# The last stage of a hybrid decoder step: tokens on partitions in five tiles, with the gate's weights as the moving operand

## The chip, the cores and the metric

One NeuronCore of a Trainium2 chip runs the whole program. The time is device microseconds (us) of one launch. Three runs of the kernel before took 2060.99, 2060.96 and 2056.74 us, with a median of 2060.96 us. A fourth, profiled run took 2059.39 us; the first to the last instruction in its trace span 2057.6 us.

The engines are named as in the profile: PE multiplies matrices (PEld is its weight load), DVE works on vectors, ACT applies functions and copies, POOL here issues gathers and some transfers, and SP issues most transfers. Each engine takes its instructions in program order, so an instruction that waits also holds whatever is queued behind it on that engine.

## What is computed

The layer runs on T = 544 tokens (512 of a prompt and 32 of decoding samples) of width 1024, all in 32-bit floats. Cut to the parts that matter here, the reference is:

```
x = x + merged @ w_out                                  # two token mixers, merged
x = x + peer_ffn(rmsnorm(x, g_ffn), ...)                # experts, 16384 of one neuron each
ple_gate = sigmoid(rmsnorm(x, g_ple) @ w_ple_gate)      # 1024 x 1024
x = x + (p @ w_ple) * ple_gate                          # p has 256 columns
y = rmsnorm(x, g_final)
```

The last three lines are the last stage, the one that the change rewrites. A matrix product of two 32-bit operands is made as three faster products: each operand is split into a rounded high part and the rest (`split`, L121: a copy by ACT to the high part, a subtraction by DVE for the low one), and high times high, low times high and high times low are added up.

## The kernel before, in words

The mixers take the first 650 us of the trace. After them, one scheduled block (line 835) holds everything else. Its program order on each engine is not the order of the source: a scheduler in the compiler's front end reorders the block's instructions by simulated times, so a change anywhere in the block can move instructions elsewhere in it.

The block has four parts. **Queries**: x1, the sum of the input and the mixers' output, lies in SBUF with channels on partitions (`x1[128, 8, 544]`). It is stored to a DRAM buffer `x1s` (L870, five transfers from POOL), normed into `hf`, split, and multiplied with 16 chunks of the query weights (L916). Of the last 128 prompt tokens and the 32 samples a token-major copy is made for the experts that are gathered (`token_rows`, L902 and L905: PE transposes of `hf`, which ACT copies into `htok` and `hsam`). Each query chunk is scored against 128 keys (`psc`, L937), and DVE picks the top 16 of each row (`top16`, from L892 on). **Gates** turn these into a dense matrix of expert weights for the first 384 tokens. **Products**: 128 blocks of experts, counted by j, each with an up product (`ublock`, L966 to L969), an activation times a gate (`act*gg`, L1180), a split into `wgh` and `wgl`, and 18 matmuls of 512 columns into three accumulators `pacc` (L1194). **Gathered experts**: for the other 160 tokens, POOL gathers rows of single experts (L1108) and DVE adds them up (`accg`, L1126), in between the products.

The last stage before, L1219 to L1313, works with channels on partitions, on two halves of 272 tokens each. x1 is loaded back (L1222, tied to the load of block 118). The first three token tiles of the experts' sum are copied out of PSUM, turned by 24 PE transposes (L1249) and added to x1 by DVE (L1251). `p @ w_ple` is 96 matmuls of 272 columns (L1265). For each half a norm is made over partitions (`rms_rstd`, L92: squares by ACT, sums by DVE, matmuls with ones and a broadcast), the normed half is split into `fh` and `fl`, and the gate is 192 matmuls of 272 columns (L1303) with the weights as the stationary operand. A chunk of weights `wpg` serves one half, so the eight chunks are loaded and split twice (16 calls of `wload`). After each chunk come the sigmoid, the product with `pw` and the sum; after each half, the last norm and four output transfers (L1313).

## Time and profile before

| | before |
|---|---|
| median of three runs | 2060.96 us |
| profiled run | 2059.39 us |
| span of its trace | 2057.6 us |
| PE busy | 1976.0 us, 96% |
| DVE busy | 1706.7 us, 83% |
| ACT busy | 1028.8 us, 50% |
| POOL busy | 513.9 us, 25% |
| from the last matmul of the experts (1957.2) to the end | 100.4 us |

All times in the trace count from the start of the span. PEclk is the clock granted to PE as a share of full speed: 1.00 is the upper of its two levels (2.4 GHz), 0.50 the lower (1.2 GHz), and numbers in between are mixes over the stretch. Where matmuls follow each other, the price of one is the distance from start to start, not its own duration, since they overlap.

### The profile page before, as it was taken

How to read it: one execution, taken by the hardware profiler on the slowest of the kernel's cores; microseconds unless marked ns; L12 is line 12 of the kernel's file. 1: busy time of each engine (PE TensorE's matmuls, PEld its weight loads, DVE VectorE, ACT ScalarE, POOL GpSimd, SP SyncE). 2: the span in 40 equal slices, each digit the busy share in tenths (PEclk: the TensorE clock that was granted, in tenths of full speed). 3: DMA queues.
4: the chain of work that ended last, by engine and by line, in shares of the span. 5: the costliest groups of instructions: out<-in, count | busy, mean ns of one | idle time of the engine just before them, and what ended most of it. 6: DMA issues, size and time to landing. Idle time of an engine off the chain costs nothing.

```text
span 2057.6 us, 34634 instructions
## 1 busy us (share of the span) xinstructions
PE 1976.0 (96%) x12292; PEld 1833.5 (89%) x12292; DVE 1706.7 (83%) x4582; ACT 1028.8 (50%) x1717; POOL 513.9 (25%) x503
## 2 busy tenths in 40 slices
PE   6899999999998999999999799999999999999986
PEld 6898988988998999999999688888888888888886
DVE  7687988886566799999999888888888888887877
ACT  5657577663534446766666333333333333343374
POOL 0001010000000001213332455543433334543500
PEclk9999999999999999999999899999999999999998
DMA  4334443445755238999999899999999998999843
GB/s 161 113 103 137 149 153 125 166 147 176 264 191 190 79 94 202 255 265 351 388 369 325 309 351 353 334 356 344 345 339 349 346 331 328 342 337 328 296 135 105
DMA packets 188364, 516.10 MB, mean 251 GB/s; under 512 B 18464, under 2 KB 71712, under 8 KB 188064
## 3 DMA queue, kind: packets, MB, share of 16 engines
q1 hardware_dynamic: 131952, 311.11, 43.5%
q0 software_dynamic: 56240, 202.80, 28.9%
q8 instruction: 96, 1.57, 0.3%
q14 instruction: 76, 0.62, 0.1%
HBM read 453.64 MB, written 60.20 MB: 250 GB/s over the span
## 4 chain that ended last, share of the span: by engine, by line
PE 86%; DVE 5%; DMA 4%; ACT 3%; issue 3%; POOL 0%; SPq 0%; DVEq 0%; ACTq 0%; POOLq 0%
PE pacc L1194 26%; PE pj L165 15%; PE pu L967 8%; PE pu L966 8%; PE pu L969 8%; PE pj L916 5%; PE pg L1083 3%; PE pj L1303 2%; DMA lraw<-in_eu 1%; PE pma L348 1%; PE pmb L553 1%; PE pmb L544 1%; ACT whi L122 1%; PE psc L937 1%; DMA usp<-lraw 1%
## 5 line engine op out<-in xcount | busy, mean ns | idle before, releaser
L966 PE MATMUL pu<-hh,whi 128*128 128x384 f32 x1024 | 346.0, 338 | 2.6 <-ACT act L977 2.6
L967 PE MATMUL pu<-hl,whi 128*128 128x384 f32 x1024 | 346.3, 338 | 0.0
L1108 POOL DMA_INDIRECT rows<-in_ev,idxs x160 | 218.0, 1362 | 267.8 <-DVE accg L1126 228.3
L123 DVE TENSOR_TENSOR wlo<-wraw,whi 128x1024 fp32r<-128x1024 f32 x172 | 210.0, 1222 | 74.6 <-ACT whi L122 65.7
L1108 POOL DMA_INDIRECT rows<-in_eur,idxs x160 | 202.1, 1263 | 248.1 <-DVE jk L1116 213.7
L122 ACT ACTIVATE whi<-wraw 128x1024 fp32r<-128x1024 f32 x172 | 181.7, 1057 | 164.2 <-PE pj L165 84.9
L1126 DVE SCALAR_TENSOR_TENSOR accg<-rows,wts,accg 128x1024 f32<-128x1024 f32 x158 | 202.5, 1281 | 21.1 <-DMA rows<-in_ev,idxs 20.9
L1194 PE MATMUL pacc<-whi,wgl 128*128 128x512 f32 x768 | 197.5, 392 | 6.1 <-DVE wgl L123 6.1
L969 PE MATMUL pu<-hh,wlo 128*128 128x384 f32 x1024 | 202.0, 336 | 0.0
L1194 PE MATMUL pacc<-whi,wgh 128*128 128x512 f32 x768 | 198.2, 394 | 2.5 <-ACT wgh L122 2.5
L966 PEld LDWEIGHTS pu<-hh,whi 128*128 128x128 f32 x1024 | 192.5, 188 | 5.8 <-ACT act L977 3.2
L1194 PE MATMUL pacc<-wlo,wgh 128*128 128x512 f32 x768 | 195.9, 390 | 0.0
L967 PEld LDWEIGHTS pu<-hl,whi 128*128 128x128 f32 x1024 | 192.7, 188 | 2.6
L122 ACT ACTIVATE whi<-vraw 128x1024 fp32r<-128x1024 f32 x128 | 134.8, 1054 | 113.9 <-PE pacc L1194 86.4
L123 DVE TENSOR_TENSOR wlo<-vraw,whi 128x1024 fp32r<-128x1024 f32 x128 | 156.6, 1224 | 36.8 <-ACT whi L122 34.4
L165 PE MATMUL pj<-xh,whi 128*128 128x272 f32 x768 | 175.8, 303 | 4.6 <-ACT sg L691 2.7
L969 PEld LDWEIGHTS pu<-hh,wlo 128*128 128x128 f32 x1024 | 178.8, 188 | 0.0
L1194 PEld LDWEIGHTS pacc<-whi,wgl 128*128 128x128 f32 x768 | 144.9, 189 | 38.0 <-DVE wgl L123 6.8
L165 PE MATMUL pj<-xh,wlo 128*128 128x272 f32 x768 | 174.9, 302 | 0.0
L165 PE MATMUL pj<-xl,whi 128*128 128x272 f32 x768 | 174.2, 301 | 0.2 <-DVE xl L123 0.2
L1194 PEld LDWEIGHTS pacc<-wlo,wgh 128*128 128x128 f32 x768 | 144.7, 188 | 30.1
L1194 PEld LDWEIGHTS pacc<-whi,wgh 128*128 128x128 f32 x768 | 144.0, 189 | 29.2 <-ACT wgh L122 2.6
(488 smaller groups left out, 4326.3 us busy)
## 6 DMA issues: line engine op xcount, KB each, us to landing
wraw<-in_eu SPq DMA_DIRECT2D x128, 512.0 KB, 6.0
vraw<-in_ev SPq DMA_DIRECT2D x128, 512.0 KB, 6.6
wraw<-in_win SPq DMA_DIRECT2D x48, 512.0 KB, 3.8
gg<-gdram SPq DMA_DIRECT2D x25, 768.0 KB, 7.6
gdram<-go SPq DMA_DIRECT2D x36, 512.0 KB, 9.8
lraw<-in_eu SPq DMA_DIRECT2D x34, 512.0 KB, 4.1
usp<-lraw SPq DMA_DIRECT2D x34, 512.0 KB, 2.6
wlo<-usp SPq DMA_DIRECT2D x34, 512.0 KB, 8.2
```

Source lines behind the costliest of these rows:

```text
L122: S.activation(hi, src, AF.Copy)
L123: return V.tensor_sub(lo, src, hi.bitcast(F32))
L165: PE.matmul(ps[:, hf, :HT], a, b[:, HS[hf]], start=(i == 0 and j == 0), stop=(i == n - 1 and j == 2))
L916: PE.matmul(p[:, i, :HT], w_[:, k], x_[:, k, :HT], start=(k == 0 and j == 0), stop=(k == 7 and j == 2))
L966: PE.matmul(ps[:, :ND], wh[:, k], hh[:, k], start=(k == 0), stop=False)
L967: PE.matmul(ps[:, :ND], wh[:, k], hl[:, k], start=False, stop=False)
L969: PE.matmul(ps[:, :ND], wl[:, k], hh[:, k], start=False, stop=(k == 7))
L1083: PE.matmul(p[:, j], A[:, j], B[:, j], start=True, stop=True)
L1108: G.indirect_dma_start(out=r, out_offset=None, in_=src, in_offset=bass.IndirectOffsetOnAxis(ap=idx, axis=0))
L1126: V.scalar_tensor_tensor(accs[i], r, wts[i][:, k:k + 1], accs[i], op0=OP.mult, op1=OP.add)
L1194: PE.matmul(pacc[t][:, hf], w_[:, ts], v_[:, hf * 512:(hf + 1) * 512], start=(j == 0 and i == 0), stop=(j == 127 and i == 2))
L1303: PE.matmul(ps, a[:, k], b[:, k], start=(k == 0 and j == 0), stop=(k == 7 and j == 2))
```

## The change

The last stage now has tokens on partitions, in four tiles of 128 tokens and one of 32. Five things follow from that.

- x1 is stored token-major. At the block's start, 40 PE transposes (`px`, in ten groups of four) turn x1 into two PSUM buffers, ACT copies each group of four into a half of `htok` or `hsam`, which serve as staging, and POOL issues ten transfers instead of five. The buffers of `px` are those that `token_rows` and the scores use afterwards, and `token_rows` writes `htok` and `hsam` only once the transfers that read them have landed.
- The experts' sum lies token-major in PSUM already, so it is added from there: no copies, no transposes.
- The gate's weights, as rows of channels, are the moving operand. They are loaded and split once (8 blocks, and 2 of `w_ple`), through two raw buffers instead of three, and stay in SBUF. A tile takes 48 matmuls of 512 columns for the gate (`pj`) and 12 for `p @ w_ple` (`pw`), so 240 and 60 in all. The stationary operand, the normed tile, must have channels on partitions, so each tile has 8 PE transposes (`pt`) behind its norm.
- A norm is one pass of ACT over 128x1024 with the sum of squares as its second output, seven small operations and one pass of DVE. The channel weights of both norms come as a new input of 1 MB (`grow`, into `gw`).
- The output leaves in five transfers, one for each tile.

The source asks for tile t+1's `pw`, norm and transposes ahead of tile t's gate. The core of the diff (left out: the pools' lines, the two halves' norm, and the arrangement of inputs and outputs on the host):

```diff
-TW = 3, 2
+TW = 2
...
-    for t in range(5):
-        G.dma_start(x1s[t, :, :, :min(128, T - t * 128)], x1[:, :, t * 128:min(T, t * 128 + 128)])
...
+    for t in range(5):
+        n = min(128, T - t * 128)
+        for i in range(2):
+            p = pst.tile([128, 4, 128], F32, name="px", tag="mx")
+            for k in range(4):
+                PE.transpose(p[:n, k], x1[:, 4 * i + k, t * 128:t * 128 + n], ident)
+            xq = (htok, hsam)[t % 2][:n, i * 512:i * 512 + 512]
+            S.activation(xq.rearrange("p (a b) -> p a b", a=4), p[:n], AF.Copy)
+            G.dma_start(x1s[t, :n, i * 512:i * 512 + 512], xq)
...
+    aps.close()
+
+    NT = (128, 128, 128, 128, NS)
+    wt = tail.enter_context(tc.tile_pool(name="wt", bufs=1, side="right", reuse_waits="tile"))
+    lp = tail.enter_context(tc.tile_pool(name="lp", bufs=2, reuse_waits="tile"))
...
+    x1 = wt.tile([128, 5, 1024], F32, name="x2")
     with tc.issue_after(loads[XL].ins):
         for t in range(5):
-            n = min(128, T - t * 128)
-            nc.sync.dma_start(x1[:, :, t * 128:t * 128 + n], x1s[t, :, :, :n])
...
+            nc.sync.dma_start(x1[:NT[t], t], x1s[t, :NT[t]])
+
+    def parts(src):
+
+        raw = tile_("wraw", TW, [128, 1024], F32, wt)
+        nc.sync.dma_start(raw, src)
+        hi = tile_("wth", 10, [128, 1024], F32R, wt)
+        lo = tile_("wtl", 10, [128, 1024], F32R, wt)
+        split(hi, lo, raw)
+        return hi, lo
+
+    ph = tile_("ph", 1, [128, 2, T], F32R, wt)
+    pl = tile_("pl", 1, [128, 2, T], F32R, wt)
+    for k in range(2):
+        raw = tile_("wraw", TW, [128, 1024], F32, wt)
+        nc.sync.dma_start(raw[:, :T], pT[:, k])
+        split(ph[:, k], pl[:, k], raw[:, :T])
+    wpl = [parts(wple[k]) for k in range(2)]
+    wgt = [parts(wpg[k]) for k in range(8)]
+    gw = tile_("gw", 1, [128, 2, 1024])
+    nc.sync.dma_start(gw, grow)
...
+    def rstd(x, n, junk):
+
+        q = tile_("rs", 4, [128, 5, 1])
+        ss, ms, rt, r, y = (q[:n, i] for i in range(5))
+        S.activation(junk, x, AF.Square, accum_out=ss)
+        V.tensor_scalar(ms, ss, 1.0 / 1024, EPS, op0=OP.mult, op1=OP.add)
+        S.activation(rt, ms, AF.Sqrt)
+        V.reciprocal(r, rt)
+
+        V.tensor_mul(y, r, r)
+        V.tensor_mul(y, y, ms)
+        V.tensor_scalar(y, y, -0.5, 1.5, op0=OP.mult, op1=OP.add)
+        V.tensor_mul(r, r, y)
+        return r
...
+    def residual(t):
+        n = NT[t]
+        for i in range(2):
+            c = slice(512 * i, 512 * i + 512)
+            if t < 3:
+                add = pacc[t][:, i]
+            elif t == 3:
+                add = accs[0][:, c]
+            else:
+                add = psu.tile([128, 512], F32, name="pts", tag="pu")[:NS]
+                PE.matmul(add, sel, accs[1][:, c], start=True, stop=True)
+            V.tensor_add(x1[:n, t, c], x1[:n, t, c], add)
+
+    def normed(t):
+
+        n = NT[t]
+        x = x1[:n, t]
+        xs = tile_("xs", 3, [128, 1024])
+        V.scalar_tensor_tensor(xs[:n], x, rstd(x, n, xs[:n]), gw[:n, 0], op0=OP.mult, op1=OP.mult)
+        hi = tile_("fh", 2, [128, 8, 128], F32R)
+        lo = tile_("fl", 2, [128, 8, 128], F32R)
+        for i in range(2):
+            p = psu.tile([128, 512], F32, name="pt", tag="pu").rearrange("p (a b) -> p a b", a=4)
+            for k in range(4):
+                c = (4 * i + k) * 128
+                PE.transpose(p[:, k, :n], xs[:n, c:c + 128], ident[:n, :n])
+            split(hi[:, 4 * i:4 * i + 4, :n], lo[:, 4 * i:4 * i + 4, :n], p[:, :, :n])
+        return hi[:, :, :n], lo[:, :, :n]
+
+    def mm_t(ps, xh_, xl_, ws):
+
+        for k, (wh, wl) in enumerate(ws):
+            for j, (a, b) in enumerate(((xh_[:, k], wh), (xl_[:, k], wh), (xh_[:, k], wl))):
+                for i in range(2):
+                    PE.matmul(ps[:, i], a, b[:, 512 * i:512 * i + 512], start=(k == 0 and j == 0),
+                              stop=(k == len(ws) - 1 and j == 2))
...
-        for k0 in range(0, 8, 4):
-            ot = ots[k0 // 4]
-            S.activation(ot, pacc[t][:, k0 // 4], AF.Copy)
-            residual(t, ot, k0)
...
-    for c in range(8):
-        wh, wl = wpl[c // 4]
-        for hf in range(2):
-            p = psu.tile([128, 512], F32, name="pw", tag="pu")
-            for k in range(2):
-                w_ = 2 * (c % 4) + k
-                for j, (a, b) in enumerate(((wh, ph), (wh, pl), (wl, ph))):
-                    PE.matmul(p[:, :HT], a[:, w_], b[:, k, HS[hf]], start=(k == 0 and j == 0), stop=(k == 1 and j == 2))
-            S.activation(pw[:, c, HS[hf]], p[:, :HT], AF.Copy)
...
-    for i, (hh, hl) in enumerate(parts):
-        for c in range(8):
-            wh, wl = wload(wpg[c])
-            ps = psj.tile([128, 512], F32, name="pj", tag="pj")[:, :HT]
-            for k in range(8):
-                for j, (a, b) in enumerate(((wh, hh), (wh, hl), (wl, hh))):
-                    PE.matmul(ps, a[:, k], b[:, k], start=(k == 0 and j == 0), stop=(k == 7 and j == 2))
-            sg = tile_("sg2", 2, [128, HT])
-            S.activation(sg, ps, AF.Sigmoid)
-            V.tensor_mul(sg, sg, pw[:, c, HS[i]])
-            V.tensor_add(x1[:, c, HS[i]], x1[:, c, HS[i]], sg)
-        xs, r3 = norm(i)
-        for k in range(0, 8, 2):
-            yo = tile_("yo", NYO, [128, 2, HT])
-            for m in range(2):
-                V.scalar_tensor_tensor(yo[:, m], xs[:, k + m], par("g_final", k + m), r3, op0=OP.mult, op1=OP.mult)
-            nc.sync.dma_start(yT[:, k:k + 2, HS[i]], yo)
...
+    psj = tail.enter_context(tc.tile_pool(name="psj2", bufs=3, space=PSUM, reuse_waits="tile"))
+
+    def embed(t):
+        n, s_ = NT[t], slice(t * 128, t * 128 + NT[t])
+        p = psj.tile([128, 2, 512], F32, name="pw", tag="pj")[:n]
+        mm_t(p, ph[:, :, s_], pl[:, :, s_], wpl)
+        pw = tile_("pw", 2, [128, 2, 512])[:n]
+        for i in range(2):
+            S.activation(pw[:, i], p[:, i], AF.Copy)
+        return pw
+
+    def last(t, pw, hi, lo):
+        n = NT[t]
+        p = psj.tile([128, 2, 512], F32, name="pj", tag="pj")[:n]
+        mm_t(p, hi, lo, wgt)
+        x = x1[:n, t]
+        for i in range(2):
+            c = slice(512 * i, 512 * i + 512)
+            sg = tile_("sg", 2, [128, 512])[:n]
+            S.activation(sg, p[:, i], AF.Sigmoid)
+            V.tensor_mul(sg, sg, pw[:, i])
+            V.tensor_add(x[:, c], x[:, c], sg)
+        yo = tile_("xs", 3, [128, 1024])[:n]
+        V.scalar_tensor_tensor(yo, x, rstd(x, n, yo), gw[:n, 1], op0=OP.mult, op1=OP.mult)
+        nc.sync.dma_start(yT[t * 128:t * 128 + n], yo)
+
+    ready = embed(0), *normed(0)
+    for t in range(5):
+        now = ready
+        if t < 4:
+            if t >= 2:
+                residual(t + 1)
+            ready = embed(t + 1), *normed(t + 1)
+        last(t, *now)```

What the scheduler makes of it is shown at three places. **SP, the end of its queue.** Before, x1's loads stand between the loads of experts' blocks, and the last stage's weights run through in one stream with the output among them:

```order
L1172 DMA vraw<-in_ev 128x1024
L1222 DMA x_13820<-x1s 128x8x128 x4
L1222 DMA x_13820<-x1s 128x8x32
L1172 DMA vraw<-in_ev 128x1024
L130 DMA wraw<-in_eu 128x1024
L1172 DMA vraw<-in_ev 128x1024 x2
```

```order
L130 DMA wraw<-in_wple 128x1024 x2
L1243 DMA yo<-in_pT 128x544 x2
L130 DMA wraw<-in_wpg 128x1024 x14
L1313 DMA out_yT<-yo 128x2x272 x4
L130 DMA wraw<-in_wpg 128x1024 x2
L1313 DMA out_yT<-yo 128x2x272 x4
```

Now (`x_20818` is x1 in the last stage):

```order
L1177 DMA vraw<-in_ev 128x1024 x2
L1255 DMA gw<-in_grow 128x2048
L1235 DMA x_20818<-x1s 128x1024 x4
L1235 DMA x_20818<-x1s 32x1024
L1250 DMA wraw<-in_pT 128x544 x2
L1240 DMA wraw<-in_wple 128x1024 x2
L1240 DMA wraw<-in_wpg 128x1024 x8
L1339 DMA out_yT<-xs 128x1024 x4
L1339 DMA out_yT<-xs 32x1024
```

All expert loads come first, then `gw`, whose space is free once DVE has made the last `wgl`; x1 follows it, and the first load of `w_ple` waits until DVE has split the first half of p.

**PE, the start of the queries**, right behind the broadcast of the second half's norm. Before:

```order
L115 MATMUL pn<-ident,rs 128x16
L916 MATMUL pj<-hh_6885,whi 128x272 x2
L902 MATMUL ph<-ident,hf 128x128 x2
L905 MATMUL ph<-ident,x_7116 128x128
L905 MATMUL ph<-ident,x_7123 128x128
L916 MATMUL pj<-hl_6886,whi 128x272
```

Now (`x_6282` is x1 there, `hh_6885` and `hl_6886` the second half's split):

```order
L115 MATMUL pn<-ident,rs 128x16
L924 MATMUL pj<-hh_6885,whi 128x272 x2
L885 MATMUL px<-ident,x_6282 128x128 x8
L924 MATMUL pj<-hl_6886,whi 128x272
L924 MATMUL pj<-hh_6885,wlo 128x272
```

Four more groups of eight `px` follow among the query matmuls, 18 to 26 rows apart, and the transposes of `token_rows` stand behind the last; the first score (`psc`) comes after all 16 of those, where before it came among them.

**DVE, the end of the experts.** Before, five additions of gathered rows stand behind the last `act*gg`:

```order
L123 TENSOR_TENSOR wgl<-act,wgh 128x384
L1126 SCALAR_TENSOR_TENSOR accg_6858<-rows,wts_6856,accg_6858 128x1024 x2
L1180 TENSOR_TENSOR act<-act,gg 128x384
L1126 SCALAR_TENSOR_TENSOR accg_6858<-rows,wts_6856,accg_6858 128x1024 x3
L123 TENSOR_TENSOR wgl<-act,wgh 128x384
L1126 SCALAR_TENSOR_TENSOR accg_6858<-rows,wts_6856,accg_6858 128x1024 x2
L1227 COPY sel<-ident 32x32 x4
```

Now none does:

```order
L123 TENSOR_TENSOR wgl<-act,wgh 128x384
L1134 SCALAR_TENSOR_TENSOR accg_6858<-rows,wts_6856,accg_6858 128x1024 x2
L1185 TENSOR_TENSOR act<-act,gg 128x384
L123 TENSOR_TENSOR wgl<-act,wgh 128x384
L1258 COPY sel<-ident 32x32 x4
L1286 TENSOR_TENSOR x_20818<-x_20818,pacc_13888 128x512 x2
```

The whole chain of additions has moved about two blocks j ahead of the products. In the last stage itself PE's order is: transposes of tile 0 and half of tile 1's, 24 `pw` matmuls, tile 0's gate mixed with 32 of tile 1's 48 gate matmuls as the weights come, `pw` of tile 2, the other 16 of tile 1, `pw` of tile 3, then transposes of tile 2, and so on tile after tile. On DVE the normed tile 2 stands behind the finished output of tile 0 and behind tile 1's sigmoid products.

## Rows read from the trace of the kernel before

**Rows 1.** The page: busy time of the engines, and the shares of the chain of waits that ended last.

```profile
PE 1976.0 (96%) x12292; PEld 1833.5 (89%) x12292; DVE 1706.7 (83%) x4582; ACT 1028.8 (50%) x1717; POOL 513.9 (25%) x503
...
PE 86%; DVE 5%; DMA 4%; ACT 3%; issue 3%; POOL 0%; SPq 0%; DVEq 0%; ACTq 0%; POOLq 0%
```

**Rows 2.** Windows of the queries, the gates and the products: stretch, its length, busy us of PE, PEld, DVE, ACT and POOL (with instructions), granted clock, DMA share, GB/s.

```profile
650.00:660.00 10.00, 5.21 (x32) 4.67 (x32) 7.29 (x17) 5.73 (x12) 2.59 (x3) 0.77 0.53 172
660.00:670.00 10.00, 8.45 (x56) 7.80 (x55) 9.43 (x23) 4.17 (x11) 0.00 (x0) 0.89 0.60 175
670.00:680.00 10.00, 8.05 (x52) 7.95 (x53) 5.16 (x17) 5.78 (x27) 0.00 (x0) 0.83 0.13 48
680.00:690.00 10.00, 9.17 (x75) 8.93 (x74) 4.58 (x9) 6.03 (x17) 0.00 (x0) 1.00 0.33 107
...
700.00:790.00 90.00, 89.91 (x718) 89.53 (x718) 90.00 (x617) 38.74 (x59) 3.74 (x5) 1.00 0.38 105
...
700.00:1900.00 1200.00, 1182.20 (x6571) 1093.20 (x6571) 1063.11 (x3390) 544.88 (x893) 434.28 (x362) 0.99 0.91 316
```

**Rows 3.** Windows of the last stage, same columns.

```profile
1957.20:2057.60 100.40, 79.47 (x576) 75.09 (x574) 74.47 (x167) 59.54 (x116) 0.00 (x0) 0.92 0.37 123
...
2044.70:2057.60 12.90, 2.26 (x12) 2.10 (x12) 5.68 (x17) 2.32 (x4) 0.00 (x0) 0.63 0.25 86
```

**Rows 4.** The chain of waits from 1940 on, in order of time: start, length, what.

```profile
1944.89 12.30 PE pacc L1194 x54
1957.21 3.67 DMA wraw<-in_wple
...
2029.54 15.17 PE pj L1303 x118
```

**Rows 5.** Timeline of PE, last stage: start, us, line, operation, count, and in brackets the idle time before it.

```profile
1957.01 1.09 PE L1249 MATMUL pt<-ident,ot 128*128 128x128 f32 x8
...
1964.49 0.52 PE L1265 MATMUL pw<-fh,whi 128*128 128x272 f32 x2 [2.98 <-ACT fh L122]
...
2023.72 0.39 PE L1303 MATMUL pj<-fh,whi 128*128 128x272 f32 x1 [1.82 <-ACT whi L122]
2023.95 0.29 PE L1303 MATMUL pj<-fl,whi 128*128 128x272 f32 x1
...
2024.46 0.43 PE L1303 MATMUL pj<-fl,whi 128*128 128x272 f32 x1
...
2027.18 0.43 PE L1303 MATMUL pj<-fl,whi 128*128 128x272 f32 x1
...
2028.23 0.29 PE L1303 MATMUL pj<-fh,wlo 128*128 128x272 f32 x1
```

**Rows 6.** Transfers from 1955 on, from issue to landing: KB each, median us.

```profile
wraw<-in_wpg SPq DMA_DIRECT2D x16, 512.0 KB, 3.5
```

**Rows 7.** x1's five loads (L1222), from issue to landing.

```profile
DMA to landing us min/median/max: 8.5/12.1/14.9
```

**Rows 8.** Timeline of ACT, last stage.

```profile
1960.90 1.06 ACT L122 ACTIVATE whi<-wraw 128x1024 fp32r<-128x1024 f32 x1 [0.20 <-DMA wraw<-in_wple]
...
1970.77 1.28 ACT L107 ACT_TABLE_LOAD   x1
1972.06 0.20 ACT L107 ACTIVATE rs<-rs 128x3 f32<-128x3 f32 x1
...
2044.73 0.40 ACT L1305 ACTIVATE sg<-pj 128x272 f32<-128x272 f32 x1 [1.15 <-PE pj L1303]
```

**Rows 9.** Timeline of DVE, end of the experts and last stage.

```profile
1947.02 0.55 DVE L1180 TENSOR_TENSOR act<-act,gg 128x384 f32<-128x384 f32 x1
1947.49 1.28 DVE L1126 SCALAR_TENSOR_TENSOR accg<-rows,wts,accg 128x1024 f32<-128x1024 f32 x1
...
1953.22 0.55 DVE L123 TENSOR_TENSOR wgl<-act,wgh 128x384 fp32r<-128x384 f32 x1
...
1955.99 1.28 DVE L1126 SCALAR_TENSOR_TENSOR accg<-rows,wts,accg 128x1024 f32<-128x1024 f32 x1 [0.70 <-DMA rows<-in_ev,idxs]
...
1957.94 1.29 DVE L1251 TENSOR_TENSOR x<-x,pt 128x512 f32<-128x512 f32 x2
...
1972.51 0.16 DVE L110 TENSOR_TENSOR rs<-rs 128x3 f32<-128x3 f32 x1
1972.71 0.16 DVE L111 TENSOR_TENSOR rs<-rs 128x3 f32<-128x3 f32 x1
...
1976.36 1.22 DVE L123 TENSOR_TENSOR wlo<-wraw,whi 128x1024 fp32r<-128x1024 f32 x1
...
2051.02 3.36 DVE L1312 SCALAR_TENSOR_TENSOR yo<-x,pkt,pn 128x272 f32<-128x272 f32 x8 [1.56 <-PE pn L115]
```

**Rows 10.** Timeline of DVE in the queries.

```profile
680.29 0.45 DVE L904 COPY x<-hf 128x128 f32<-128x128 f32 x2 [5.14 <-PE ph L905]
...
685.97 0.57 DVE L904 COPY x<-hf 128x128 f32<-128x128 f32 x2 [2.37 <-PE ph L905]
689.05 1.22 DVE L123 TENSOR_TENSOR wlo<-wraw,whi 128x1024 fp32r<-128x1024 f32 x1 [2.50 <-PE ph L902]
693.69 0.88 DVE L892 MAX8 vals<-sc 128x8 f32<-128x128 f32 x4 [3.42 <-ACT sc L938]
```

73 lines of the change are left out of this document (13 added, 60 removed).

## The prediction

> **What bounds the kernel now.** I read the page first. PE is busy 96% of the span and has 86% of the chain that ended last [rows 1], so PE's stream is the bound nearly everywhere, and a change pays or costs by what it does to that stream. Next I read windows, since a mean over the span hides the two stages that the change touches. From 700 to 1900 PE is busy 1182 of 1200 us [rows 2]: what delays the start of this stretch is carried to its end. In 650 to 690 PE has 9.1 us of idle time (40 less 5.21, 8.45, 8.05 and 9.17) [rows 2], and there the changed store of x1 falls. The last stage takes 100.4 us, of which PE is busy 79.5 [rows 3]; of its 20.9 us idle, 10.6 lie behind the last gate matmul, in the last norm and the output. So in the last stage PE is still the main term, but a quarter of the time belongs to waits.
>
> Four prices follow from rows. A matmul of 512 columns costs 12.30 / 54 = 0.228 us, one of 272 columns 15.17 / 118 = 0.129 [rows 4], a transpose 1.09 / 8 = 0.136 [rows 5]. The granted clock falls after a wait: behind the 1.82 us of idle time at 2023.72, with other gaps just before it, matmuls of 272 columns start 0.227 apart from 2024.46 to 2027.18 (12 of them) and 0.126 apart later [rows 5], which is the lower level and costs some 1.5 us.
>
> **The front: x1 stored token-major.** It adds 40 transposes, 40 x 0.136 = 5.4 us on PE, and ten copies by ACT, which is half idle there [rows 2]. All 40 stand behind the second half's norm, at 671.8 and later on the clock of before, where PE has only some 2.8 us of idle time up to 690 [rows 2], so at least 2.6 us are new. Each group of four also waits until ACT has emptied one of two buffers, and `token_rows` behind them waits until the transfers that read `htok` and `hsam` have landed; five groups of eight at some 0.6 us of waiting is 3 us. DVE's first top 16 starts at 693.69, after waits of 5.14, 2.37, 2.50 and 3.42 us for PE's transposes and scores [rows 10], and from 700 to 790 DVE is busy for all of the 90 us, as PE is [rows 2]. By the new order the first score comes after all transposes, which I put about 10 us later, at 703. DVE can make up only what it idles today. A stretch in which both engines are full takes over a shift nearly whole, whichever of the two leads. The store's own transfers go through POOL, which has nothing else there, so ten instead of five cost nothing on the path. I take +6 us. The lower bound is 0 (all hidden in the 9.1 us), the upper 10 (DVE's shift whole).
>
> **The middle.** Here the order is the same up to block 117 or so. x1's loads leave the stream of expert loads, where they took 8.5 to 14.9 us to land [rows 7]; PE is full there, so I cost that at nothing, as the cover is PE's own queue. The gather chain moves forward by two blocks, about 12 us; its price is a rival below.
>
> **The last stage, step by step,** counted from the end of the last expert matmul at 1957.2 [rows 4].
>
> 1. *Start.* PE has nothing until tile 0 is normed. DVE adds the experts' sum (0.645 for each half tile [rows 9]), so tile 0 takes 1.3; ACT squares it in 1.06, the time of a copy of 128x1024; table load 1.28 and square root 0.2 [rows 8] follow, up to 1961.2, while DVE adds tiles 1 and 2. Behind these on DVE stand tile 3's sum (1.3), eleven small operations of two norms at 0.2 from start to start [rows 9], a split of p (0.7) and the norm's pass (1.28, as `accg` [rows 9]): 5.5 us. First transposes at about 1966.9, against 1964.5 for the first `pw` today [rows 5]. This needs x1 by 1957: `gw` and x1 go out when the last `wgl` is done, at 1950 without the additions before it, and 1.5 MB have 7 us, twice the 3.5 of 0.5 MB [rows 6]. Bounds: 6 us of idle time (today's 7.3, less a little) to 13 (x1 three us late).
> 2. *Weights.* The first `w_ple` load waits for p's split, so it goes out near 1965.5. With two raw buffers, a pair of weights takes one landing (3.67 [rows 4]), one copy (1.06 [rows 8]), one subtraction (1.22 [rows 9]) and two handovers: 6.1 us. Five pairs put the last weight at 1965.5 + 30.5 + 1.2 = 1997.2. Up to there PE has 116 matmuls, 26.4 us, and 12 transposes, 1.6: it keeps step and idles some 2 us. Tile 0's gate ends near 1998.5. That a pair lands slower is a rival.
> 3. *The rest of PE's work:* 184 matmuls (16 of tile 1, 24 `pw`, 144 of tiles 2 to 4) at 0.228 are 42.0, 24 transposes 3.3, two matmuls with `sel` about 1. Sum 46.3, so 2044.8 without waits. The fifth tile has 32 tokens and costs as much as one of 128, since the columns set the price.
> 4. *Waits in between.* Tile 2's transposes need its norm, which stands on DVE behind tile 1's sigmoid products and tile 0's output. Tile 1's gate ends near 2002; then come two sigmoids (1.1), a table load and two roots (1.7), half a sum (0.65), ten small operations (2.0) and two passes (2.56): 2010. PE has 12 `pw` matmuls (2.7) in that time, so it waits 5.3 us, and about 1 more for the split. I take 2 us for tile 4's turn, none for tile 3's. Sum 8.3, bounds 2 and 12. The low clock behind the long wait costs 1.5.
> 5. *End.* From the last gate matmul: two sigmoids 1.0, half a product and sum 1.3, square 1.06, table load and root 1.5, six small operations 1.2, a pass 1.28, and the output's 3.2 us as today (from 2054.4, where the last `yo` ends [rows 9], to 2057.6): 10.5, against 12.9 today [rows 3].
>
> The end is 1957.2 + 9.7 + 31.6 + 46.3 + 8.3 + 1.5 + 10.5 = 2065.1, against 2057.6: +7.5. PE's work alone tells why: 300 x 0.228 = 68.4 us of matmuls take the place of 480 x 0.129 = 61.9.
>
> On the table loads, a page speaks against this change. The Trainium skill (ScalarE: Activation LUTs, "What ACT_TABLE_LOAD costs") adds to the 1.28 us of a load a drain of about 1.38 us at every switch; the changed stage has nine switches between root and sigmoid, and by that, an estimate from the page, the three on my path would put the end 4 us later. The trace disagrees: the root starts at 1972.06, right behind the load of 1970.77 to 1972.05 [rows 8].
>
> **Sum.** 7.5 + 6 = 13.5. On the profiled run's own 2059.4 us that is 2073 us; that run lies 1.6 us below the median of 2061, within the spread of the runs.
>
> **Rivals.**
> *Fewer waits on PE (faster).* The changed stage has 76 us of work for PE (68.4, 40 transposes 5.4, some 1 for `sel`, low clock 1.5). It beats today's 100.4 as soon as its idle time is under 24 us. I walked 30.5: 9.7 at the start, 2 for weights, 8.3 in between, 10.5 at the end. If the start falls to 5 because p's split and tile 0's norm come first in time, and tile 2's norm overlaps with tile 1's gate, 17 remain, and the stage takes 93 us; with the front hidden in the 9.1 us [rows 2] the run is 2052. For it: the weights are split ten times instead of 18, on engines that the gate waits for today [rows 5]. Against it: DVE takes its queue in order, and PE cannot do tile 2 without it. Chance 0.20.
> *The gather chain is late.* `act*gg` of the last block stands behind every addition now. It starts at 1947.02 today, with five additions behind it that end at 1957.3, each waiting for its rows [rows 9]. If the gathers set that pace whatever the order, `act*gg`, `wgl`, the last 18 matmuls and x1's loads all come later, by up to 8 us: 2081. It decides as soon as the last addition ends after 1947. For it: the waits for rows; against it: x1's loads no longer press on the gathers. Chance 0.12.
> *A low clock while weights come.* In windows where PE is busy 52% to 85%, the granted clock is 0.77 to 0.89, at 92% it is 1.00 [rows 2]. With waits for every pair from 1967 to 1998, PE may stay on the lower level for much of it, 116 matmuls cost up to 53 us instead of 26, and the stage becomes PE's: +10, 2083. The Trainium skill (TensorE: Matmul & The Clock Gate, "HAM oscillation — how this bites in real kernels") describes this for loops that wait for a load before each burst. No row before has such a stretch. Chance 0.10.
> *Two raw buffers starve the stream.* If a pair lands in 6 us instead of 3.7, five pairs cost 11 us more: 2084. Chance 0.08. That weights are still loaded twice is excluded by the order.
>
> **How the numbers follow.** The forecast has 0.50, at 2073 us (2064 to 2082 with its own bounds). About 0.2% or 4 us is what can be told from no change here. Of the forecast's half, 0.40 is slower by more, 0.08 within, 0.02 faster; of the first rival's 0.20, 0.14 is faster and 0.06 within; the other three (0.30) are slower but for 0.02. So faster 0.16, same 0.16, slower 0.68. The range of 2055 to 2087 leaves out the faster rival's better half and the worst of the slower ones.
>
> **What would show it.** Right, if DVE's first top 16 starts near 700 or later and the last expert matmul ends about 6 us later than 1957; if PE idles some 10 us behind that matmul; if weights come in pairs of 6 us; if PE waits 5 us or more between tile 1's gate and tile 2's transposes. Wrong in the front, if the top 16 starts at 694 as before; wrong in the last stage, if it takes under 100 us, with idle time on PE under 24.

## The result and the profile after

The changed kernel takes 2073.39 us, the median of 7 runs (2065.48 to 2078.15), against 2060.42 us before (2056.4 to 2060.99, 7 runs): ratio 1.0062, 95% interval 1.0045 to 1.0079. On another chip, beside later runs, the same program gave 1.0079 (1.0059 to 1.01). By these two, the change makes the kernel slower by 13.0 us (2073.39 - 2060.42) and by 16.5 (2075.13 - 2058.66). Its profiled execution took 2076.81 us with a span of 2075.0.

The page first, to be held against [rows 1]:

```profile
PE 1982.2 (96%) x12100; PEld 1819.1 (88%) x12100; DVE 1690.6 (81%) x4542; ACT 1025.0 (49%) x1691; POOL 516.0 (25%) x508
...
PE 86%; DVE 6%; DMA 3%; issue 3%; ACT 2%; POOL 0%; SPq 0%; ACTq 0%; DVEq 0%; POOLq 0%
```

PE has 192 instructions fewer and is busy 6 us longer, and the span is 17.4 us longer: some 11 us are time in which PE stands. Where, the windows say. Queries, the full stretch, and the last stage of the changed kernel with two windows of its own (columns as in [rows 2]):

```profile
670.00:680.00 10.00, 8.11 (x68) 8.15 (x69) 4.83 (x15) 7.58 (x26) 2.15 (x4) 1.00 0.28 105
680.00:690.00 10.00, 9.72 (x79) 9.39 (x79) 2.74 (x5) 6.23 (x11) 3.15 (x6) 1.00 0.63 216
690.00:700.00 10.00, 8.42 (x66) 7.62 (x65) 3.94 (x9) 5.03 (x19) 0.00 (x0) 1.00 0.29 94
700.00:790.00 90.00, 89.77 (x722) 89.17 (x723) 90.00 (x614) 36.38 (x59) 2.70 (x3) 1.00 0.34 96
700.00:1900.00 1200.00, 1178.45 (x6569) 1089.62 (x6570) 1068.19 (x3423) 545.39 (x896) 437.29 (x363) 0.99 0.90 313
1964.90:2075.00 110.10, 82.75 (x344) 59.40 (x344) 56.58 (x121) 51.14 (x81) 0.00 (x0) 0.85 0.23 83
...
1970.00:1980.00 10.00, 6.00 (x20) 4.93 (x21) 8.51 (x19) 4.72 (x7) 0.00 (x0) 0.50 0.40 143
1980.00:1990.00 10.00, 10.00 (x46) 8.09 (x45) 5.11 (x6) 5.61 (x8) 0.00 (x0) 0.97 0.48 173
```

From 680 to 700 DVE is busy only 6.7 of 20 us, while PE has the transposes and the query products behind them; from 700 on both engines are full as before, so the delay is kept. The last stage takes 110.1 us, of which PE is busy 82.75, at a mean clock of 0.85; it was 100.4, 79.5 and 0.92 [rows 3].

The front on PE and DVE (timeline, idle time and its releaser in brackets). PE's five groups of transposes, then DVE's waits up to the first top 16, which began at 693.69 before [rows 10]:

```profile
671.89 1.07 PE L885 MATMUL px<-ident,x 128*128 128x128 f32 x8 [1.97 <-DVE x L912]
675.42 1.04 PE L885 MATMUL px<-ident,x 128*128 128x128 f32 x8
679.06 1.03 PE L885 MATMUL px<-ident,x 128*128 128x128 f32 x8
683.61 1.03 PE L885 MATMUL px<-ident,x 128*128 128x128 f32 x8
687.26 1.04 PE L885 MATMUL px<-ident,x 128*32 128x128 f32 x8
```

```profile
680.22 1.23 DVE L123 TENSOR_TENSOR wlo<-wraw,whi 128x1024 fp32r<-128x1024 f32 x1 [5.40 <-ACT whi L122]
...
689.99 1.23 DVE L123 TENSOR_TENSOR wlo<-wraw,whi 128x1024 fp32r<-128x1024 f32 x1 [5.98 <-ACT whi L122]
...
699.86 0.87 DVE L900 MAX8 vals<-sc 128x8 f32<-128x128 f32 x4 [1.93 <-ACT sc L946]
```

The last stage: SP's queue (issues of a line), then all of PE's idle time in it.

```profile
1958.28 2.69 SPq L1235 DMA_DIRECT2D x<-x1s  x5
1961.02 4.23 SPq L1250 DMA_DIRECT2D wraw<-in_pT  x2
1972.05 2.22 SPq L1240 DMA_DIRECT2D wraw<-in_wple  x2
1977.85 20.77 SPq L1240 DMA_DIRECT2D wraw<-in_wpg  x8
```

```profile
1973.34 1.97 PE L1300 MATMUL pt<-ident,xs 128*128 128x128 f32 x8 [8.45 <-DVE xs L1293]
1975.96 1.11 PE L1300 MATMUL pt<-ident,xs 128*128 128x128 f32 x4 [0.66 <-DVE fl L123]
2018.79 1.94 PE L1300 MATMUL pt<-ident,xs 128*128 128x128 f32 x8 [6.18 <-DVE rs L1265]
2052.21 0.65 PE L1309 MATMUL pj<-wth,fh 128*32 128x512 f32 x2 [0.74 <-ACT fh L122]
2053.08 0.65 PE L1309 MATMUL pj<-wth,fl 128*32 128x512 f32 x2 [0.22 <-DVE fl L123]
```

PE stands for 16.2 us inside the stage, 8.45 of it for tile 0's norm and 6.18 for tile 2's; the weights `w_ple` go out 11 us behind the two halves of p that fill both raw buffers, and those of the gate then go out over 20.8 us. Twelve `pw` matmuls behind the wait for tile 2 take 4.33 us in the chain of waits of this kernel (twelve take 2.80 in that of the run four_raw, shown below):

```profile
2006.17 0.61 ACT sg L1334
...
2011.52 0.97 ACT sg L1334 x2
...
2018.79 1.94 PE pt L1300 x8
...
2021.78 4.33 PE pw L1309 x12
...
2053.08 10.81 PE pj L1309 x46
2063.91 0.59 ACT sg L1334
```

### The profile page after: what moved, and what is told of

Same layout as the page of the kernel before. It is cut to its first block, busy times and chain, and to the rows that moved or that the text cites. A ratio compares the mean times of both kernels' runs of the same rounds, so it can differ in the third digit from the quotient of the medians.

```text
span 2075.0 us, 34137 instructions
## 1 busy us (share of the span) xinstructions
PE 1982.2 (96%) x12100; PEld 1819.1 (88%) x12100; DVE 1690.6 (81%) x4542; ACT 1025.0 (49%) x1691; POOL 516.0 (25%) x508
## 3 DMA queue, kind: packets, MB, share of 16 engines
q8 instruction: 95, 1.56, 0.3%
## 4 chain that ended last, share of the span: by engine, by line
PE 86%; DVE 6%; DMA 3%; issue 3%; ACT 2%; POOL 0%; SPq 0%; ACTq 0%; DVEq 0%; POOLq 0%
PE pacc L1199 25%; PE pj L165 15%; PE pu L975 8%; PE pu L974 8%; PE pu L977 8%; PE pj L924 4%; PE pg L1091 3%; PE pj L1309 3%; PE pmb L553 1%; PE pma L348 1%; PE pmb L544 1%; PE psc L945 1%; PE pw L1309 1%; DMA usp<-lraw 1%; DMA rows<-in_ev,idxs 1%
## 5 line engine op out<-in xcount | busy, mean ns | idle before, releaser
L974 PE MATMUL pu<-hh,whi 128*128 128x384 f32 x1024 | 345.8, 338 | 2.6 <-ACT act L985 2.6
L123 DVE TENSOR_TENSOR wlo<-wraw,whi 128x1024 fp32r<-128x1024 f32 x154 | 188.1, 1221 | 79.3 <-ACT whi L122 72.8
L122 ACT ACTIVATE whi<-wraw 128x1024 fp32r<-128x1024 f32 x154 | 162.8, 1057 | 154.7 <-PE pj L165 84.6
L1134 DVE SCALAR_TENSOR_TENSOR accg<-rows,wts,accg 128x1024 f32<-128x1024 f32 x158 | 202.4, 1281 | 14.7 <-DMA rows<-in_ev,idxs 14.5
L977 PE MATMUL pu<-hh,wlo 128*128 128x384 f32 x1024 | 202.0, 336 | 0.0
L974 PEld LDWEIGHTS pu<-hh,whi 128*128 128x128 f32 x1024 | 192.4, 188 | 5.8 <-ACT act L985 3.2
L122 ACT ACTIVATE whi<-vraw 128x1024 fp32r<-128x1024 f32 x128 | 134.9, 1055 | 117.5 <-PE pacc L1199 108.7
L123 DVE TENSOR_TENSOR wlo<-vraw,whi 128x1024 fp32r<-128x1024 f32 x128 | 156.6, 1224 | 36.9 <-ACT whi L122 34.2
L977 PEld LDWEIGHTS pu<-hh,wlo 128*128 128x128 f32 x1024 | 178.8, 188 | 0.0
## 6 DMA issues: line engine op xcount, KB each, us to landing
wraw<-in_eu SPq DMA_DIRECT2D x128, 512.0 KB, 6.2
vraw<-in_ev SPq DMA_DIRECT2D x128, 512.0 KB, 6.4
wraw<-in_win SPq DMA_DIRECT2D x48, 512.0 KB, 3.7
gdram<-go SPq DMA_DIRECT2D x36, 512.0 KB, 9.3
lraw<-in_eu SPq DMA_DIRECT2D x34, 512.0 KB, 4.0
usp<-lraw SPq DMA_DIRECT2D x34, 512.0 KB, 2.6
wlo<-usp SPq DMA_DIRECT2D x34, 512.0 KB, 7.6
```

The source lines that it names most:

```text
L122: S.activation(hi, src, AF.Copy)
L123: return V.tensor_sub(lo, src, hi.bitcast(F32))
L974: PE.matmul(ps[:, :ND], wh[:, k], hh[:, k], start=(k == 0), stop=False)
L977: PE.matmul(ps[:, :ND], wl[:, k], hh[:, k], start=False, stop=(k == 7))
L1134: V.scalar_tensor_tensor(accs[i], r, wts[i][:, k:k + 1], accs[i], op0=OP.mult, op1=OP.add)
```

## The experiments

Two lengths are read from every profile. *Front*: from the start of the mixers' last addition to x (L828, the same in all kernels) to the start of DVE's first top 16. *Stage*: from the end of the last expert matmul to the end of the span. *Products* is the time from that same addition to the end of the last expert matmul, so it contains the front. The mixers' end itself lay between 642.6 and 654.6 us in these profiles, before any changed instruction, so spans and single times are not compared. Ratios are to the kernel before, run beside each kernel on the same chip.

| kernel | ratio, 95% interval | front | products | stage |
|---|---|---|---|---|
| before | | 40.65 | 1304.13 | 100.43 |
| before_again | 1.0005 (0.9989 to 1.0021) | 40.66 | 1304.51 | 100.76 |
| after | 1.0062 (1.0045 to 1.0079) | 47.84 | 1312.87 | 110.11 |
| after_again | 1.0079 (1.0059 to 1.01) | 49.35 | 1314.39 | 110.35 |
| front_only | 1.0023 (1.001 to 1.0036) | 48.43 | 1312.78 | 101.33 |
| no_front | 1.0045 (1.0029 to 1.0062) | 40.66 | 1306.98 | 109.20 |
| px_only | 1.0072 (1.0049 to 1.0095) | 45.22 | 1310.67 | 109.48 |
| early_x | 1.0082 (1.0063 to 1.0101) | 46.57 | 1314.21 | 110.22 |
| two_ahead | 1.0066 (1.0049 to 1.0083) | 49.39 | 1311.45 | 105.79 |
| four_raw | 1.0043 (1.003 to 1.0056) | 49.40 | 1314.15 | 100.56 |
| best | 1.0028 (1.0014 to 1.0042) | 46.53 | 1312.02 | 101.10 |
| four_tiles | 0.9978 (0.9963 to 0.9993) | 49.43 | 1311.78 | 87.25 |
| no_front_four | 0.9997 (0.998 to 1.0013) | 40.66 | 1304.39 | 100.39 |
| late_x | 1.0021 (1.0007 to 1.0035) | 40.65 | 1305.2 | 106.0 |

The theory: two separate costs, the transposes of x1 in the queries and the waits of the last stage. The rivals: one of them costs all, or the last stage loses by its larger matmul work alone.

**before_again, after_again.** Copies of the two kernels, for second profiles.

> The kernel before once more, for a second profile of it beside the others: if the two lengths belong to the kernel, first search 40 to 42 us behind the mixers' last add (40.65 in the first profile) and last stage 99.5 to 101.5 us (100.43); time within 0.2% of before. If they scatter by several us, the lengths of single profiles tell nothing.

> The changed kernel once more, beside the others on one chip, for a second profile of it. If the lengths of front and stage belong to the kernel and not to one execution: first search 47 to 49 us behind the mixers' last add (47.84 in the first profile), last stage 109 to 111 us (110.11), whatever the mixers' end does, which lay at 642.6 to 654.6 us in the profiles so far; time 1.0045 to 1.008 of before. If they scatter as the mixers' end does, by several us, then the differences of 4 to 10 us in the other runs tell nothing.

The lengths repeat to 0.4 us before, to 1.5 us after. The 1.5 us go with the clock: in the five us from 20 us behind the mixers' last addition it is 1.00 in the first profile (front 47.84) and 0.66 to 0.70 in after_again, two_ahead, four_raw and four_tiles, whose fronts are 49.35 to 49.43. The products scatter more, 1311.45 to 1314.39 among these five; the one long wait there, PE's for the first `wgl`, is 5.50 us in two_ahead, 7.85 in after_again and 8.38 in the first profile. Differences of 4 us or more in one profile can be read.

**front_only.** The kernel before, with the transposes and copies added, storing to memory that nobody reads:

```diff
         G.dma_start(x1s[t, :, :, :min(128, T - t * 128)], x1[:, :, t * 128:min(T, t * 128 + 128)])
...
+            p = pst.tile([128, 4, 128], F32, name="px", tag="mx")
+                PE.transpose(p[:n, k], x1[:, 4 * i + k, t * 128:t * 128 + n], ident)
+            S.activation(xq.rearrange("p (a b) -> p a b", a=4), p[:n], AF.Copy)
+            G.dma_start(x1t[t, :n, i * 512:i * 512 + 512], xq)
```

> The kernel before, with the change's front added and nothing else: x1 is also turned by 40 PE transposes, copied by ACT and stored token-major by ten more transfers to a buffer that nothing reads; the last stage is the old one. Theory (the front costs PE and DVE time that the full stretch behind it carries to the end): 2060.4 + 7 = 2067 us, 2064 to 2070, with the first top 16 of DVE 6 to 10 us later than at 693.7. Rival (the front is hidden in PE's idle time around 650 to 690, and the whole loss of 13 us arises in the last stage): 2060 to 2062 us.

2063.92 us against 2058.24: +5.7, or 2.1 to 7.4 by the interval of the ratio. The front is 7.8 us longer, the products end 8.6 later, and the stage is that of before within 0.9. The front alone costs, and carries to the end.

**no_front.** The changed kernel without the transposes; x1 is stored by five plain transfers, so the last stage adds x1 in a wrong order, with the same work:

```diff
+    for t in range(5):
+        src = x1[:, :, t * 128:t * 128 + 128] if t < 4 else x1[:NS, :, :128]
+        G.dma_start(x1s[t, :min(128, T - t * 128)], src)
...
-            p = pst.tile([128, 4, 128], F32, name="px", tag="mx")
```

> The changed kernel without its front: x1 is stored straight from SBUF by five transfers as before, and the last stage loads these bytes as if they were token-major, so it adds x1 in a wrong order; every other step is the changed kernel's. Theory: the front's 6 to 8 us go, the last stage keeps its 7 to 10 us over the kernel before: 2066 us, 2063 to 2070. Rival (all 13 us arise in the last stage): 2073 us, as the changed kernel.

2065.55 against 2058.24: +7.3, with a front of 40.66 and a stage of 109.20. The two parts add within the noise: 5.7 + 7.3 = 13.0, where the change itself costs 13.0 us on one chip and 16.5 on another. That the sum fits the first to a tenth is luck, since the interval of no_front is 6.0 to 12.8 us, and four_raw below, which has the front and a stage as long as before, costs 9.2 us on the same chip. (The products of this profile, 1306.98, are 2.8 us longer than before, though the first matmul into `pacc` starts 501.6 us behind the addition as before; then PE waits 8.23 us for the first `wgl`, against 6.12. It is the scatter named above, so they are not used.)

**px_only.** no_front, with the transposes back at their place, but without copies and stores (x1 in the wrong order again):

```diff
+            p = pst.tile([128, 4, 128], F32, name="px", tag="mx")
+            for k in range(4):
+                PE.transpose(p[:n, k], x1[:, 4 * i + k, t * 128:t * 128 + n], ident)
```

> The changed kernel with the 40 transposes of x1 at their place, but without the ten copies that read them and without their stores; the residual is stored by five plain transfers in the wrong order, so the last stage adds a wrong residual. Theory A (the front costs PE's own time, because PE is the engine that sets the pace there): 40 x 0.13 = 5.2 us, so the first search 45 to 47 us behind the mixers' last add (40.66 without the transposes, 47.84 to 49.35 with all), ratio to before 1.0065 to 1.008 where it was 1.0045 without them. Theory B (the copies on ACT and the two token buffers that their stores free late): the search within 1.5 us of 40.66, ratio 1.004 to 1.0055.

The front is 4.6 us longer than no_front's, of 7.2 to 8.7 with copies and stores: most of it is PE's own time, 5 x 1.04 us by the timeline after, and the rest comes with the copies. Theory A holds for the front; the interval of the ratio is too wide to add to it. What px_only saves against the full change, 4.1 us at the top 16 against after_again, isn't kept: a tenth of the up products (L974 to L977) is reached 194.9 us behind the addition in both (187.3 before). PE waits 2.79 us for `act` at 821, where after_again waits 1.70, and has a clock of 0.72 and then 0.60 in the ten us there, where after_again has 1.00.

**early_x.** The transposes moved ahead of the norm, where PE idles, with two PSUM banks of their own:

```diff
+    psx = psx_s.enter_context(tc.tile_pool(name="psx", bufs=2, space=PSUM, reuse_waits="tile"))
+            p = psx.tile([128, 4, 128], F32, name="px", tag="mx")
...
+    psx_s.close()
     first = [wload(wq[c]) for c in range(2)]
```

> The changed kernel with one edit: the 40 transposes of x1 and their ten copies stand ahead of the norm behind the mixers and have two PSUM banks of their own, so that they need not wait behind the norm's product and can run while DVE closes the last residual adds. Theory A (the transposes and copies cost because they stand between the norm and the scores on PE and ACT): the first top-16 search of token tile 0 comes 41 to 44 us behind the mixers' last add (40.65 before, 47.84 changed), and the kernel is 3 to 6 us faster than the changed one, near 2060 to 2063 where before is 2058 to 2060. Theory B (PE's and ACT's time there is short in sum, wherever the 9 us of transposes stand): the search stays 46 to 49 us behind, and the time within 1 us of the changed kernel's, 2064 to 2066 for a no-front kernel plus 5.

Theory A of this run fell: front 46.57, in the range of theory B, and no faster. The transposes do run where PE idled, but of their some 8 us only 1.3 to 2.9 are saved at the top 16 (46.57 for 47.84 to 49.43) and 0.3 to 1.7 at the first matmul into `pacc` (507.5 us behind the addition for 507.7 to 509.2); at the products' end (1314.21) none is seen. Windows of early_x, and one line of PE's timeline:

```profile
650.00:660.00 10.00, 4.75 (x28) 3.25 (x26) 9.79 (x20) 9.02 (x20) 2.65 (x5) 0.78 0.68 228
660.00:670.00 10.00, 7.77 (x34) 6.28 (x33) 4.88 (x15) 4.17 (x9) 2.69 (x6) 0.50 0.81 272
```

```profile
667.39 0.59 PE L928 MATMUL pj<-hh,whi 128*128 128x272 f32 x1 [1.91 <-ACT htok L879]
```

DVE is busy 9.8 and ACT 9.0 of the ten us from 650 to 660: PE's idle time there was the norm's, and the copies now stand on ACT beside it. PE then waits 1.91 us for the last copies, and runs at the lower level (0.50) from 660 to 670, where it had 0.84 in the changed kernel (whose mixers end 2 us later). Which of the two keeps the saving so small is not shown.

**two_ahead.** Norm and embedding two tiles ahead of the gate instead of one:

```diff
-    ready = embed(0), *normed(0)
+    ready = [(embed(0), *normed(0)), (embed(1), *normed(1))]
...
+            ready.append((embed(t + 2), *normed(t + 2)))
```

> The changed kernel, with the embedding product, norm and transposes of a tile asked for two tiles ahead of its gate instead of one (a third buffer for the normed tile's two parts and for the embedding product, a fourth for the norm's output). Theory (PE waits 6.2 us for tile 2's norm, because it stands on DVE and ACT behind tile 0's output, and then runs some 4 us on the lower clock): the wait and the low clock behind it go, 2073.4 - 7 = 2066 us, 2063 to 2069. Rival (the wait only moves, to weights that are not there yet or to the end): 2072 to 2074 us.

The wait of 6.18 us for tile 2 is gone and the stage is 4.3 us shorter, but new gaps of 1.31 and 2.25 us open while weights come. The time, 2070.36 us, lies between the theory and the rival, and the ratio can't be told from that of the changed kernel.

**four_raw.** Four raw weight buffers for two:

```diff
-TW = 2
+TW = 4
```

> The changed kernel with four raw buffers for the last stage's weights instead of two. Theory (a load waits until the weight two before it is split, so two raw buffers set the pace of 3 us per weight that PE follows from 1977 to 2004): weights come up to 8 us earlier, and PE, which has 28 us of work for these 27 us plus some on the lower clock, gains 2 to 4 us: 2070 us, 2068 to 2072. Rival (PE's own work sets the pace there): 2073 us, no change.

2067.42 against 2058.24, and the stage falls by 9.5 us to 100.56, that of before. SP's queue and all of PE's idle time in this stage:

```profile
1957.41 4.30 SPq L1250 DMA_DIRECT2D wraw<-in_pT  x2
1961.75 0.91 SPq L1240 DMA_DIRECT2D wraw<-in_wple  x2
1968.52 12.79 SPq L1240 DMA_DIRECT2D wraw<-in_wpg  x8
```

```profile
1969.80 1.97 PE L1300 MATMUL pt<-ident,xs 128*128 128x128 f32 x8 [8.46 <-DVE xs L1293]
2009.09 0.73 PE L1309 MATMUL pj<-wth,fh 128*128 128x512 f32 x2 [0.79 <-ACT fh L122]
2039.05 0.65 PE L1309 MATMUL pj<-wth,fh 128*32 128x512 f32 x2 [0.73 <-ACT fh L122]
2039.92 0.65 PE L1309 MATMUL pj<-wth,fl 128*32 128x512 f32 x2 [0.22 <-DVE fl L123]
```

The wait for tile 2 vanished too, so the stage gains more than the 2 to 4 us expected. One number was edited, but the scheduler has also put the stage in another order. In the changed kernel PE makes 32 of tile 1's 48 gate matmuls among those of tile 0, and ACT and DVE take tile 1's sigmoid and its products (L1334, L1335) ahead of the root and the pass of tile 2's norm (L1266, L1293). In four_raw PE makes tile 0's gate first and then all of tile 1's, and tile 2's norm stands ahead of tile 1's sigmoid. ACT and DVE, first of the changed kernel, then of four_raw (last weight split, sigmoids of tiles 0 and 1, tile 1's products, tile 2's norm), and PE's chain in four_raw:

```profile
2001.85 1.06 ACT L122 ACTIVATE wth<-wraw 128x1024 fp32r<-128x1024 f32 x1 [1.99 <-DMA wraw<-in_wpg]
...
2006.17 1.09 ACT L1334 ACTIVATE sg<-pj 128x512 f32<-128x512 f32 x2 [1.96 <-PE pj L1309]
2011.43 1.06 ACT L1334 ACTIVATE sg<-pj 128x512 f32<-128x512 f32 x2
2012.51 1.28 ACT L1266 ACT_TABLE_LOAD   x1
2013.80 0.29 ACT L1266 ACTIVATE rs<-rs 128x1 f32<-128x1 f32 x2
...
2012.04 1.29 DVE L1335 TENSOR_TENSOR sg<-sg,pw 128x512 f32<-128x512 f32 x2 [0.33 <-ACT sg L1334]
...
2017.37 1.28 DVE L1293 SCALAR_TENSOR_TENSOR xs<-x,rs,gw 128x1024 f32<-128x1024 f32 x1
```

```profile
1985.76 1.06 ACT L122 ACTIVATE wth<-wraw 128x1024 fp32r<-128x1024 f32 x1 [0.30 <-DMA wraw<-in_wpg]
...
1993.05 1.09 ACT L1334 ACTIVATE sg<-pj 128x512 f32<-128x512 f32 x2 [4.93 <-PE pj L1309]
...
2004.67 1.09 ACT L1334 ACTIVATE sg<-pj 128x512 f32<-128x512 f32 x2 [3.37 <-PE pj L1309]
...
2002.31 1.29 DVE L1293 SCALAR_TENSOR_TENSOR xs<-x,rs,gw 128x1024 f32<-128x1024 f32 x1
...
2005.31 1.29 DVE L1335 TENSOR_TENSOR sg<-sg,pw 128x512 f32<-128x512 f32 x2 [1.71 <-ACT sg L1334]
```

```profile
1993.47 11.16 PE pj L1309 x48
2004.64 2.80 PE pw L1309 x12
```

Counted from the start of tile 0's sigmoid, tile 2's norm is done after 12.5 us in the changed kernel (2006.17 to 2018.65) and after 10.5 in four_raw (1993.05 to 2003.60). In that time PE has 6.4 us of work there, the other 16 gate matmuls of tile 1 and 12 `pw` (to 2012.6), and 14.2 us here, 48 and 12 (to 2007.26). So 12.5 - 6.4 = 6.1 us are the wait of 6.18, and here none is left. Some 2 us of it are the order on ACT and DVE, and the larger part, by these lengths, is that both gates end with the weights: the sigmoids start 5.3 us apart with two buffers and 11.6 with four. Whether earlier weights would do it in the old order, or the new order with late weights, no run shows.

**best.** early_x and four_raw together, tile 0's norm ahead of the other tiles' additions and squares, and the square-root table loaded while the last products run:

```diff
+            S.activation(lt.tile([128, 1], F32, name="warm"), a[:, 0:1], AF.Sqrt, scale=0.0)
...
+        with tc.issue_after(norms[0].ins) if len(norms) == 1 else ExitStack():
...
+            with tc.issue_after(firsts[0].ins) if t else ExitStack():
```

> The transposes early as in early_x, four raw weight buffers in place of two, tile 0's norm kept ahead of the other tiles' residual adds and tile 1's squares, and the square-root table loaded while the last expert's products still run. If the three costs are separate, they add up: front 0 to 3 us over before, start of the last stage with PE idle some 5 us in place of 8.45, stage 96 to 98 us (100.43 before, 100.56 with four raw buffers alone), so the kernel is 0 to 4 us faster than before, 2055 to 2060 where before is 2058 to 2060. Rival: what PE no longer waits for at the start it waits for at the weights (first pw with wple's second half, gate products with wpg), the stage stays near 100 us and the kernel is 1 to 4 us slower than before.

The rival came true for the stage: PE's wait for tile 0 falls from 8.46 to 4.59 us, then it waits 2.76 for `wth` of `w_ple`, and the clock in the ten us from 8.7 us behind the experts' end is 0.70, where four_raw has 0.78; the stage is no shorter. The front, 46.53, misses the 0 to 3 us over before as well, so the kernel is 5.9 us slower than before (2064.59 against 2058.66).

**four_tiles.** four_raw without the fifth tile in the last stage (the 32 sample tokens' gate, embedding and norms are left out):

```diff
-    for t in range(5):
+    for t in range(4):
```

> Changed kernel with four raw weight buffers, and the fifth tile (the 32 sample tokens) left out of the last stage: its 60 matmuls (48 gate, 12 embedding), its transposes and its norms are not done, and its rows are written as they were loaded. Theory A (with the weights in time, PE's stream sets the stage, and a tile of 32 tokens costs as many columns as one of 128): the stage falls by 60 x 0.228 = 13.7 us, from 100.6 to 86 to 88 us. Theory B (matmuls with 32 rows of output are cheaper, or the tile lies beside waits): the stage falls by less than 7 us.

The stage falls by 100.56 - 87.25 = 13.3 us, near the 13.7 of theory A. With the weights in time PE's columns set the pace, and 32 tokens cost as much as 128: in the chain of the changed kernel the last 46 gate matmuls of the short tile take 10.81 us, 0.235 each.

**no_front_four.** no_front with four raw buffers (x1 in the wrong order):

> Both suspected costs taken out at once: no transposes of x1 (the residual is stored as it lies, so it is added in the wrong order), and four raw weight buffers in place of two. If the front and the raw buffers are all that the change costs, the time is that of before: ratio 0.9985 to 1.0015, search at 40.65 us, stage at 100 to 101 us. Rival: something of the change is left that neither run showed by itself, ratio above 1.002.

Ratio 0.9997 (0.998 to 1.0013); front, products and stage are those of before within 0.3 us. Beyond the interval of some 3 us either way nothing of the change is left besides these two costs, and without them the new layout gains nothing. The rival of the larger matmul work falls too: PE is busy 79.1 us in this stage, against 79.5 before [rows 3].

**late_x.** four_raw, with x1 stored by five plain transfers as before and transposed in the last stage, for tiles 0 to 2 by matmuls with `ident` that add to the experts' sums in PSUM:

```diff
+        G.dma_start(x1s[t, :, :, :min(128, T - t * 128)], x1[:, :, t * 128:min(T, t * 128 + 128)])
...
+                PE.matmul(p[:, k * 128:k * 128 + 128], xc[t][:, 4 * i + k, :n], ident, start=t == 3, stop=t == 3 or k == 3)
```

> The changed kernel with four raw weight buffers, and x1 stored channel-major by five plain transfers as in the kernel before; the 40 transposes stand in the last stage, where PE adds 24 of them into the experts' sums in PSUM while it would idle for tile 0's norm, and the other 16 with tiles 3 and 4. If it is the place of the transposes that costs the front its 8 us, the first search comes 40.66 us behind the mixers' last add as in the kernel before, the stage takes 100.56 (four raw buffers) plus 8 x 0.136 = 1.1 for tile 0 and 16 x 0.136 = 2.2 for the last two tiles, 101 to 104 us, and the kernel is 1 to 4 us slower than before: ratio 1.0005 to 1.002, against 1.0043 for four raw buffers alone. Rival: x1 is needed by PE now and lands as late as in the changed kernel, and the norms wait behind it, stage 106 us or more, ratio 1.003 or above.

The front is 40.65 and the products end as before: it was the place. The stage is 106.0, 2 us over the range expected, and the reason isn't the rival's. PE, first work behind the experts:

```profile
1959.40 5.83 PE L1280 MATMUL pacc<-ident,xc 128*128 128x128 f32 x48
1967.06 0.74 PE L1307 MATMUL pw<-wth,ph 128*128 128x512 f32 x2 [1.83 <-ACT wth L122]
```

The 24 products with `ident` count 48 instructions and take 5.83 us, 0.24 each where a transpose takes 0.13. They start right behind the experts, so x1 is there in time for them. The 16 others take some 3.2 us, and PE's idle time inside the stage falls from 10.2 us in four_raw to 6.5: 5.8 + 3.2 - 3.7 = 5.3, which is the difference of 106.0 to 100.56. At 1.0021, 4.9 us by the medians, this form costs least of those that compute the whole reference, though best (1.0028) can't be told from it; none of them beat the kernel before.

## Why the prediction was right, point by point

The time (2073 predicted, 2073.39 measured) and the sign held, and all signs named for it are there: the top 16 at 699.86, the products' end 7.7 us later (1964.9 for 1957.2), PE idle 8.45 us behind them, the eight gate weights issued over 20.8 us, so 5.9 for a pair, and 6.18 us between tile 1's gate and tile 2's transposes, in a stage of 110 us. That the total fits to 0.4 us is partly luck. Runs of the kernel spread over 12.7 us, the same program costs 16.5 us on the other chip, and the two terms of the sum were both too small: by lengths the front is 7.2 to 8.7 us and the stage 9.7, where 6 and 7.5 were predicted.

- *The front.* Predicted +6 (0 to 10). By the lengths 7.2 to 8.7 at the top 16, 6.2 to 7.7 at the first matmul into `pacc` and 6.9 to 10.3 at the products' end, with the scatter of 3 us in it; by front_only's time 5.7. The mechanism held: the shift was kept through the full stretch. px_only gives 4.6 of it at the top 16 to the transposes, near the 40 x 0.136 = 5.4 that the prediction set against PE's idle time. The step "at least 2.6 us are new" was too mild: of the 2.8 us of idle time, 1.97 lie ahead of the first transpose in both kernels (671.95 before, 671.89 after) and take none of them up. Nor did the idle time further ahead help much in early_x.
- *Start, step 1.* 9.7 predicted, 8.45 measured.
- *Weights, step 2.* From the issue of `w_ple` to the last weight 31.7 us predicted, 32.1 measured (1972.05 to 2004.17, where the last `wtl` ends); tile 0's gate predicted to end 41.3 us behind the experts (1998.5 - 1957.2), its sigmoid starts after 41.3 (2006.17 - 1964.89).
- *The rest, step 3.* The sum counts 36 transposes with step 2; the order has 40. Four of them are some 0.5 us.
- *Waits, step 4.* 5.3 + 1 predicted for tile 2, 6.18 measured; 2 for tile 4, 0.96 measured. Both halves of the prediction's reason hold: DVE's order, and that PE has little left to do behind tile 1's gate, which ends soon after tile 0's. What it left out is where they come from. With four buffers the scheduler's order and the weights' pace both change, and the wait is gone. So raw buffers, which stood among the rivals with a landing time of 6 us as their condition, account for 9.5 of the stage's 9.7 us although a weight lands in 3.4 to 4.1 us, against 3.5 before [rows 6].
- *Low clock.* 1.5 us predicted, and this is the term that was mis-sized. Behind the wait for tile 2, 12 `pw` cost 4.33 instead of 2.80, eight transposes 1.94 instead of 1.04, two gate matmuls 1.05 instead of 0.46: 3.0 us. At the start the granted clock is 0.50, the lower of the two levels, from 1970 to 1980, and the first 20 `pw`, from 1977.08 on, take 6.34 instead of 20 x 0.228 = 4.56.
- *End.* 10.5 predicted, 11.1 measured (2063.91 to 2075.0).
- *Table loads.* The Trainium skill (ScalarE: Activation LUTs, "What ACT_TABLE_LOAD costs") adds a drain of about 1.38 us to a switch. The trace disagrees after the change as before it: the load of 1.28 us starts at 2012.51 and the root at 2013.80.

The rivals: the late gather chain fell (the last `act*gg` starts at 1953.84 and its `wgh` waits for PE, not for gathered rows). The low clock while weights come fell but for its first ten us (0.50 from 1970 to 1980): from 1980 to 1990 PE is busy 10.0 us at 0.97, with `pw` and tile 1's matmuls between the weights. Fewer waits on PE fell for the change as made; with four raw buffers the stage reaches the old length, and best, which also shortened the start, no less than that. Its condition, idle time under 24 us, is met by four_raw with 21.4 us, and the stage is still no shorter: PE is busy 79.2 us there, not the 76 that this rival took.
